# A decoder block's value projection in seven products instead of eight, with weight sums by adding DMAs

## The chip, the cores and the metric

The kernel runs on one core of a Trainium2 chip. The metric is the device time of the program in microseconds. Engines of a core: TensorE (PE, with its weight loads shown as PEld), VectorE (DVE), ScalarE (ACT), GpSimd (POOL) and the queue engine SyncE (SP), which here only issues DMAs.

## The reference

One layer with 512 tokens of width 1024, in float32. A combined input projection `h @ w_in` feeds three groups of heads: A, six heads of dilated attention; B, four heads of gated linear attention in chunks; C, six heads of block-sparse attention.

```
h = RMSNorm(x)
aq, ak, av, bq, bk, bv, br, ba, cq, ck, cv = split(h @ w_in)
y_a = dilated_attention(aq, ak, av)        # 6 heads of 64
y_b = gla(bq, bk, bv, br, ba)              # 4 heads; output gate: norm(o) * silu(br)
y_c = moba_attention(cq, ck, cv)           # 6 heads of 64
x = x + concat(y_a, y_b, y_c) @ w_out
x = x + relu(RMSNorm(x) @ w_ff1)^2 @ w_ff2
out = RMSNorm(x)
```

The part that the change touches is the projection to the values and to the gate, `h @ [av | br half 0]` and `h @ [cv | br half 1]`: 512 tokens by 1024 inputs by two groups of 512 columns (384 of values and 128 of gate each). RMSNorm's row factor (rstd) is applied to the result, and the norm's weights to x.

## The kernel before

Every large product is done in three: both operands are split into a rounded part and a remainder (`xh`, `xl` for x; `wh`, `wl` for a weight piece of 128 rows by 1024 columns), and high times high, low times high and high times low are added in PSUM. ACT makes the rounded part, DVE the remainder (`parts`, line 284; `cut`, line 302, goes through the pieces in the order in which they are fetched). SP fetches them (`fetch`, line 268) and also the bias rows of the softmax (`nb`, `attention`, line 721).

The program is in stages. `first` (line 533) projects group B's q, k, v and low-rank gate. Then `main` (line 1331) runs `v_proj(0)` (values of A and half of the gate), three `qk_proj` pairs, `v_proj(1)` (values of C, the other half), three more pairs, the out-projection, and a feed-forward part in which every unit is done in Strassen's form: seven products of halves instead of eight (the table `PRODUCTS`), with the sums of weights made by DMAs that add to what lies in SBUF (issued by POOL) or by DVE. Beside `main` run `gla` (line 550), `attention` and `values` (line 784), which fill in between.

`v_proj(g)` (line 858) waits for four weight pieces, and for each of four token tiles adds 8 x 3 products of 128x512 into one of the two "mm" banks (`vps`). `v_out` (line 843) reads it twice on ACT: values `v`, and gate `rg`, from which DVE makes `sg` and `rg`; `gate` (line 919) turns them into the swish gate.

In `gla`, `levels` makes for seven block lengths L = 64, 32, ..., 1 an array `kq`; the products of its blocks (`lp`, two levels at a time, in the banks s, s, pt, pt) are copied into `attn` under a mask by DVE (`copy_predicated`). `carry` has two small PE steps, `dps` (read into `dg` by ACT) and `ktp` (the transposed keys, read into `kend`), both in "mm" banks. Then come per chunk the state update `up`, in bank g, and the output `op`, in bank o. `zps` is the gate's low-rank product, from `alT`, the transposed projection.

The order of all instructions is set by `Plan` (line 107): every stream of work is a generator that yields instructions, waits for named events, and takes and gives back resources (PSUM banks by tag, `raw` slots for fetched pieces, `w` for split pairs, `big` for 4 KB buffers). The planner keeps a clock for each engine by rough costs and always issues the instruction that could start first, with a priority for ties. What it decides is a fixed order on each engine; at run time every engine goes through its own in order and waits on semaphores.

In the profile every instruction has the planner's line 129, so groups are told apart by tile names.

Of the kernel before, what the change touches and what calls it, by code (L numbers as in the profile page):

```python
# [9 lines left out]
F32 = mybir.dt.float32  # L10
# [189 lines left out]
def hybrid_block_kernel(ctx: ExitStack, tc: tile.TileContext, xT_d, x_d, w0_d, wv_d, wqk_d, wo_d, w1_d, w2_d,  # L200
# [9 lines left out]
    plan = Plan(nc, dict(BANKS, raw=3, w=WPAIRS, big=BIGS, raw2=3, part=5, lev=4, cnt=1))  # L210
# [28 lines left out]
    nw2 = consts.tile([128, KT], F32)  # L239
    hsel = consts.tile([128, 4], F32)  # L240
# [21 lines left out]
    loaded = {}  # L262
    raws = {}
# [4 lines left out]
    def fetch():  # L268
        for key, src, n in pieces:
            if key[0] == "x":  # L270
                yield SP.dma_start(xT[key[1]], src)
                fire(("x", key[1]))
                continue
            if key[0] == "x3":
                x3[key[1:]] = slot("x3")
                yield SP.dma_start(x3[key[1:]], src)
                continue
# [24 lines left out]
    def cut():  # L302
        for key, src, n in pieces:
            if key[0] in ("x", "x3"):
                continue
            yield ("wait", ("raw", key))
            yield from parts(key, raws.pop(key), n)
            give("raw")
            give("big")

    units = [(i, c) for c in range(NC) for i in (1, 2)]
# [203 lines left out]
    G = []  # L515
# [34 lines left out]
    def gla():  # L550
# [43 lines left out]
        for l0 in range(0, len(LEVELS), 2):  # L594
# [32 lines left out]
        for n in range(NB):  # L627
            vb = vB[n // 2][:, n % 2, :]
            sold = smk
            if n < NB - 1:  # L630
                yield ("take", "g")
                up = bank("g", "up")
# [6 lines left out]
                give("g")  # L639
# [6 lines left out]
            yield ("take", "o")  # L646
            op_ = bank("o", "op")
# [5 lines left out]
            give("o")  # L653
# [189 lines left out]
    def v_out(g, t, acc):  # L843

        v = vS[g, t] = slot("v", shape=(128, 384))
        yield ACT.activation(v, acc[:, :384], AF.Copy, scale=rstd[:, t:t + 1])
# [3 lines left out]
        yield ACT.activation(rg, acc[:, 384:], AF.Copy, scale=nrstd[:, t:t + 1])  # L850
        give("mm")
        yield ("prio", 2)
        yield DVE.tensor_scalar(sg, rg, 80.0, None, op0=OP.min)
        yield DVE.tensor_tensor(rg, rg, gw[:, cs], op=OP.mult)
        if g and t % 2:
            spawn(gate(t // 2), 2)

    def v_proj(g):
        if not gates:
            gates.extend(tuple(slot(x, shape=(128, 2, 256)) for x in ("sg", "rg")) for _ in range(2))  # L860
        hl = []
        for c in range(4):
            yield ("wait", ("w", ("v", g, c)))
            hl.append(loaded.pop(("v", g, c)))
        for t in range(NT):
            yield ("take", "mm")
            acc = bank("mm", "vps")
            ts = slice(t * 128, (t + 1) * 128)
            for k in range(KT):
                wh, wl = hl[k // 2]  # L870
                w_ = slice((k % 2) * 512, (k % 2) * 512 + 512)
                yield [PE.matmul(acc, xx[:, ts], ww[:, w_], start=(k + j == 0), stop=(k == 7 and j == 2))
                       for j, (xx, ww) in enumerate(((xh[k], wh), (xl[k], wh), (xh[k], wl)))]
                if t == NT - 1 and k % 2:
                    give_w()
            if t == 0:
                yield ("wait", "rstd")
                yield ("wait", "consts")
            spawn(v_out(g, t, acc), 0.5)
# [39 lines left out]
    def gate(i):  # L919
# [10 lines left out]
        G.append(rg.rearrange("p t c -> p (t c)"))  # L930
        if i:
            fire("G")

# [413 lines left out]
    for c in range(4):  # L1347
        piece(("v", 0, c), wv_d[0, c])
    for i in range(2):
        piece(("qk", 0, i), wqk_d[i])  # L1350
    for p in (1, 2):
        for i in range(2):
            piece(("qk", p, i), wqk_d[2 * p + i])
    for c in range(4):
        piece(("v", 1, c), wv_d[1, c])
    for p in range(3, 6):
# [8 lines left out]
    def start():  # L1365
# [9 lines left out]
        yield DVE.tensor_scalar(nw2, nw[:, 1], -0.5, None, op0=OP.mult)  # L1375
        yield ("take", "mm")
# [11 lines left out]
    for k in range(KT):  # L1388
        spawn(scaled_x(k), 2)
    spawn(main(), 9)  # L1390
# [82 lines left out]
```

## Time and profile before

| | |
|---|---|
| median of 3 runs | 580.21 us (579.4 to 581.09) |
| the profiled execution | 579.58 us, span of its records 577.8 us |
| granted clock of TensorE | 0.995 |
| PE busy | 566.3 us, 98% |
| DVE busy | 446.6 us, 77% |
| ACT busy | 346.7 us, 60% |
| POOL busy | 53.6 us, 9% |

Stages by the records: the first projection to 29.4 us; `vps` of `v_proj(0)` from 33.5 to 64.7, with the first levels between; `qkps` of three pairs to 115.7; `vps` of `v_proj(1)` to 147.3; three pairs to 198.5; out-projection to about 250; the feed-forward part to the end. The page gives busy shares over the whole span; the answers by window give them for one stage. A matmul's length is its time in the pipeline, 0.39 us for 512 columns, and neighbours overlap, so steps are taken from one start to the next.

### The profile page before, as it was taken

The numbers are of one execution on the slowest core, as the hardware profiler recorded it, in microseconds if no ns is written. First come the engines' busy times: TensorE is split into PE (matmuls) and PEld (weight loads), VectorE is DVE, ScalarE is ACT, GpSimd is POOL, SyncE is SP. The second block draws the span as 40 slices with busy tenths as digits, with TensorE's granted clock in tenths as the row PEclk, the third lists the DMA queues.
The fourth block names the chain that finished last, engine by engine and source line by source line (L and its number), as shares of the span: only waits on it lengthen the run. The fifth ranks groups of instructions, "written<-read, shape, count | busy, mean of one in ns | idle before, by whom it ended". The sixth has DMA issues, their size and how long they took to land.

```text
span 577.8 us, 9359 instructions
## 1 busy us (share of the span) xinstructions
PE 566.3 (98%) x3561; PEld 487.3 (84%) x3561; DVE 446.6 (77%) x795; ACT 346.7 (60%) x601; POOL 53.6 (9%) x73
## 2 busy tenths in 40 slices
PE   9999999999999999999999999999999999999994
PEld 8967888768876778889988799988899888999884
DVE  6799976654796843759799797799975799957993
ACT  6563327646666762558785456865467764579543
POOL 4020000000000010011102002021020120011202
PEclk9999999999999999999999999999999999999998
DMA  8922233040423742378977738978269684395812
GB/s 294 399 76 74 74 111 87 23 146 5 129 87 127 274 110 37 133 220 203 205 222 149 183 111 177 296 121 231 86 150 287 149 166 161 110 218 110 147 38 109
DMA packets 27357, 87.16 MB, mean 151 GB/s; under 512 B 3360, under 2 KB 3402, under 8 KB 27312
## 3 DMA queue, kind: packets, MB, share of 16 engines
q1 hardware_dynamic: 19872, 61.15, 31.0%
q0 software_dynamic: 7152, 25.14, 23.9%
q8 instruction: 28, 0.46, 0.3%
q10 hardware_dynamic: 288, 0.27, 0.1%
q14 instruction: 17, 0.14, 0.1%
HBM read 84.42 MB, written 2.13 MB: 150 GB/s over the span
## 4 chain that ended last, share of the span: by engine, by line
PE 85%; DVE 7%; ACT 3%; DMA 2%; issue 1%; ACTq 0%; DVEq 0%
PE f1X L129 13%; PE f2X L129 12%; PE qkps L129 12%; PE vps L129 8%; PE ops L129 7%; PE f1Z L129 7%; PE f2Z L129 6%; PE f1Y L129 3%; PE f2Y L129 3%; PE sps L129 3%; DMA wraw<-in_w 2%; PE po L129 2%; PE ptp L129 2%; PE av L129 2%; DVE wl L129 2%
## 5 line engine op out<-in xcount | busy, mean ns | idle before, releaser
L129 DVE TENSOR_TENSOR wl<-wraw,wh 128x1024 fp32r<-128x1024 f32 (+1 forms) x148 | 175.1, 1192 | 36.4 <-ACT wh L129 35.9
L129 ACT ACTIVATE wh<-wraw 128x1024 fp32r<-128x1024 f32 (+1 forms) x147 | 149.3, 1032 | 51.9 <-DMA wraw<-in_w 17.4
L129 PE MATMUL f1X<-yp,wh 128*128 128x256 f32 x512 | 92.6, 283 | 0.0
L129 POOL DMA_DIRECT2D wraw<-in_w x46 | 40.5, 977 | 468.2 <-DVE wl L129 229.3
L129 PEld LDWEIGHTS f1X<-yp,wh 128*128 128x128 f32 x512 | 80.1, 192 | 0.3
L129 PE MATMUL f1X<-yp,wl 128*128 128x256 f32 x256 | 72.5, 283 | 0.2 <-DVE wl L129 0.2
L129 PE MATMUL f2X<-wl,Ah 128*128 128x512 f32 (+1 forms) x132 | 50.6, 384 | 0.1
L129 PE MATMUL f2X<-wh,Ah 128*128 128x512 f32 (+1 forms) x132 | 50.6, 383 | 0.0
L129 PE MATMUL f2X<-wh,Al 128*128 128x512 f32 (+1 forms) x132 | 50.6, 383 | 0.0
L129 PEld LDWEIGHTS f1X<-yp,wl 128*128 128x128 f32 x256 | 49.1, 192 | 0.4 <-DVE wl L129 0.4
L129 PE MATMUL f1Z<-yp,wh 128*128 128x256 f32 x256 | 46.6, 284 | 0.3 <-DVE yp L129 0.3
L129 ACT ACTIVATE h<-h 128x512 f32<-128x512 f32 x56 | 34.9, 626 | 11.9 <-DVE h L129 11.1
L129 PE MATMUL qkps<-xh,wh 128*128 128x512 f32 x96 | 40.9, 426 | 0.0
L129 PEld LDWEIGHTS f1Z<-yp,wh 128*128 128x128 f32 x256 | 40.0, 192 | 0.5 <-DVE yp L129 0.5
L129 PE MATMUL qkps<-xh,wl 128*128 128x512 f32 x96 | 37.6, 392 | 0.0
L129 PE MATMUL qkps<-xl,wh 128*128 128x512 f32 x96 | 37.5, 391 | 0.0
L129 ACT ACTIVATE P<-P,mn 128x512 f32<-128x512 f32 (+3 forms) x48 | 26.5, 553 | 17.6 <-DVE mn L129 17.6
L129 ACT ACTIVATE Ah<-h 128x512 fp32r<-128x512 f32 x40 | 24.2, 620 | 20.5 <-DVE h L129 20.5
L129 PE MATMUL f1Z<-yp,wl 128*128 128x256 f32 x128 | 36.2, 283 | 0.0
L129 DVE TENSOR_TENSOR Al<-h,Ah 128x512 fp32r<-128x512 f32 x40 | 26.9, 685 | 4.0 <-ACT Ah L129 4.0
L129 PEld LDWEIGHTS f2X<-wl,Ah 128*128 128x128 f32 x132 | 24.8, 188 | 5.4 <-DVE wl L129 0.5
L129 PEld LDWEIGHTS f2X<-wh,Ah 128*128 128x128 f32 x132 | 24.8, 188 | 4.8
(226 smaller groups left out, 1200.2 us busy)
## 6 DMA issues: line engine op xcount, KB each, us to landing
wraw<-in_w SPq DMA_DIRECT2D x66, 512.0 KB, 4.4
wraw<-in_w POOLq DMA_DIRECT2D x46, 512.0 KB, 6.4
wraw<-in_wqk SPq DMA_DIRECT2D x12, 512.0 KB, 6.6
wraw<-in_wv SPq DMA_DIRECT2D x8, 512.0 KB, 6.7
wraw<-in_wo SPq DMA_DIRECT2D x8, 512.0 KB, 5.8
nb<-tab SPq DMA_DIRECT2D x12, 256.0 KB, 4.0
wraw<-in_w SPq DMA_DIRECT2D x8, 264.0 KB, 6.7
xT<-in_xT SPq DMA_DIRECT2D x8, 256.0 KB, 6.7
```

What stands on the lines that cost most here:

```text
L129: getattr(getattr(self.nc, op.eng), op.method)(*op.args, **op.kw)
```

## The change

The two `v_proj` become one, in Strassen's form with the table that the feed-forward part has: x halved by tokens (256) and by inputs (512), the weights by inputs and by group. Seven products of 2 x 4 x 3 matmuls take the place of eight. Stage order: first, qk pairs 0 and 1, values and gate, qk pairs 2 to 5.

- The sums of x (`x_sums`, new) are made by ACT and DVE in "big" buffers and split into `xsh` and `xsl`.
- The sums of weights are made by POOL's adding DMAs: `fetch_v` loads ten pieces, `v_plus` adds eight times, `cut_v` splits fourteen.
- `v_out` adds products into `v` on DVE, or starts it on ACT, and makes the gate's two arrays from the finished `v`.
- `copy_predicated` is kept for L <= 16; for L = 64 and 32 ACT copies the blocks, one or two instructions for each head.
- `up` and `op` take "pt" banks instead of g and o, since the products hold o and g.

```
@@ gla
-                    yield DVE.copy_predicated(o4, mk, src)
+                    if L >= 32:
+                        for j in range(m):
+                            rows = slice(2 * L * j, 2 * L * j + L)
+                            yield ACT.activation(o4[rows, :, j], src[rows, :, j], AF.Copy)
+                    else:
+                        yield DVE.copy_predicated(o4, mk, src)
...
-                yield ("take", "g")
-                up = bank("g", "up")
+                yield ("take", "pt")
+                up = bank("pt", "up")
...
-            yield ("take", "o")
-            op_ = bank("o", "op")
+            yield ("take", "pt")
+            op_ = bank("pt", "op")
@@ new functions
+    def v_plus(n, ip, t, q):
+        yield POOL.dma_start(t, wv_d[q[1], 2 * q[0] + ip], accum_op=OP.add)
+        VB[n, ip] = t
+        fire(("vB", n, ip))
+
+    def fetch_v():
+        for n, q, more in ((0, (0, 0), None), (1, (1, 0), None), (3, (0, 0), (0, 1)), (5, (1, 1), None), (4, (0, 1), (1, 1))):
+            for ip in range(2):
+                yield ("take", "rawv")
+                yield ("take", "big")
+                VB[n, ip] = t = big("wraw")
+                yield SP.dma_start(t, wv_d[q[1], 2 * q[0] + ip])
+                if more:
+                    spawn(v_plus(n, ip, t, more), 3)
+                else:
+                    fire(("vB", n, ip))
+
+    def cut_v():
+        for n, *_ in PRODUCTS:
+            if n == 2:
+                yield ("prio", 1.5)
+            for ip in range(2):
+                yield ("wait", ("vB", n, ip))
+                t = VB[n, ip]
+                yield from parts(("v", n, ip), t)
+                if n in (3, 2):
+                    spawn(v_plus(*((2, ip, t, (1, 1)) if n == 3 else (6, ip, t, (1, 0)))), 3)
...
+    def x_sums():
...
+        for m in range(4):
+            yield ACT.activation(block(s, m), xT[4 + m][:, 256:], AF.Copy, scale=nnw[:, 4 + m:5 + m])
+        for m in range(4):
+            yield DVE.scalar_tensor_tensor(block(s, m), xT[m][:, 256:], nw[:, 0, m:m + 1], block(s, m), op0=OP.mult, op1=OP.add)
+        yield from parts_of(3, s)
...
@@ v_out
+            yield DVE.scalar_tensor_tensor(v, acc, (nrstd if g else rstd)[:, t:t + 1], v, op0=OP.mult, op1=OP.add)
...
+        yield DVE.tensor_scalar(sg, v[:, 384:], -1.0, 80.0, op0=OP.mult, op1=OP.min)
+        yield DVE.scalar_tensor_tensor(rg, v[:, 384:], -1.0, gw[:, cs], op0=OP.mult, op1=OP.mult)
@@ main
-        yield from v_proj(0)
-        yield from qk_proj(0)
-        yield from qk_proj(1)
-        yield from qk_proj(2)
-        yield from v_proj(1)
-        for p in range(3, 6):
+        for p in range(2):
+            yield from qk_proj(p)
+        yield from v_proj()
+        for p in range(2, 6):
             yield from qk_proj(p)
```

How the instructions stand now, at the places of which the prediction speaks. DVE, where the low-rank gate of group B is made (`la` is the log of the gate, `b` its running sum, from which the levels start); before:

```order
L129 TENSOR_SCALAR Rn_96<-rps 128x512
L129 COPY vals<-vt 12x320
L129 COPY alT<-alps 16x512
L129 COPY vals<-vt 12x320
L129 TENSOR_TENSOR wl<-wraw,wh 128x1024
L129 TENSOR_SCALAR la<-zps,bav 128x512
L129 TENSOR_TENSOR kB<-bk,R 128x512
L129 SCALAR_TENSOR_TENSOR qB<-bq,R 128x512
L129 TENSOR_TENSOR wl<-wraw,wh 128x1024
L129 TENSOR_TENSOR la<-la,ab 128x512
L129 SCALAR_TENSOR_TENSOR b<-smask,la 128x512
```

and after:

```order
L129 COPY alT<-alps 16x512
L129 TENSOR_TENSOR tq<-qkps,Rn_97 128x512
L129 TENSOR_TENSOR wl<-wraw,wh 128x1024
L129 TENSOR_TENSOR q_535<-tq,q_535 128x512
L129 TENSOR_SCALAR la<-zps,bav 128x512
L129 TENSOR_TENSOR kB<-bk,R 128x512
L129 SCALAR_TENSOR_TENSOR qB<-bq,R 128x512
L129 TENSOR_TENSOR la<-la,ab 128x512
L129 TENSOR_TENSOR wl<-wraw,wh 128x1024
L129 TENSOR_TENSOR tk<-qkps,R 128x512
L129 SCALAR_TENSOR_TENSOR b<-smask,la 128x512
```

The reads of the first qk pair (`tq`, `q`, `tk`) now stand between; ahead of this piece stand the sums of x as well.

ACT, between the levels' exponentials `e` and `dg`; before:

```order
L129 ACTIVATE eq<-b 128x512
L129 ACTIVATE e<-e 128x512 x2
L129 ACTIVATE dg<-dps 128x16
L129 ACTIVATE e<-e 128x512
L129 ACTIVATE v<-vps,rstd 128x384
L129 ACTIVATE rg<-vps,nrstd 128x128
L129 ACTIVATE kend<-ktp 128x384
```

and after:

```order
L129 ACTIVATE e<-e 128x512
L129 ACTIVATE attn_596<-lp 64x4x64
L129 ACTIVATE attn_597<-lp 64x4x64
L129 ACTIVATE attn_598<-lp 64x4x64
L129 ACTIVATE attn_599<-lp 64x4x64
L129 ACTIVATE attn_596<-lp 32x4x32 x2
L129 ACTIVATE attn_597<-lp 32x4x32 x2
L129 ACTIVATE attn_598<-lp 32x4x32
L129 ACTIVATE e<-e 128x512
L129 ACTIVATE attn_598<-lp 32x4x32
L129 ACTIVATE attn_599<-lp 32x4x32 x2
L129 ACTIVATE dg<-dps 128x16
```

The twelve copies of the first two levels stand ahead of `dg`.

SP, from the end of the first projection's loads on; before:

```order
L129 DMA wraw<-in_wv 128x1024 x4
L129 DMA wraw<-in_wqk 128x1024 x6
L129 DMA wraw<-in_wv 128x1024
L129 DMA nb<-tab 128x512 x2
L129 DMA wraw<-in_wv 128x1024 x3
```

and after:

```order
L129 DMA wraw<-in_wqk 128x1024 x4
L129 DMA wraw<-in_wv 128x1024 x10
L129 DMA wraw<-in_wqk 128x1024 x3
L129 DMA nb<-tab 128x512 x6
L129 DMA wraw<-in_wqk 128x1024 x5
```

The bias rows `nb` of the first three pairs stand behind all loads for the values and three of the next qk pieces.

More of the change, by code (lines that the diff above doesn't have):

```diff
@@ L262, in hybrid_block_kernel @@
     loaded = {}
+    VB = {}
     raws = {}
@@ L276, in fetch @@
                 yield SP.dma_start(x3[key[1:]], src)
+                continue
+            if key == "v":
+                yield from fetch_v()
                 continue
@@ L305, in cut @@
                 continue
+            if key == "v":
+                yield from cut_v()
+                yield ("prio", 3)
+                continue
             yield ("wait", ("raw", key))
@@ L514, in hybrid_block_kernel @@
     st = {}
-    G = []
+    G = {}
+    gated = [0, 0]
     mh, ml = [None] * 8, [None] * 8
@@ L652, in gla @@
             yield DVE.tensor_tensor(oB[n // 2][:, n % 2, :], op_[:, :256], dv.rearrange("p h v -> p (h v)"), op=OP.add)
-            give("o")
+            give("pt")
         yield ("wait", "G")
@@ L841, in dense, with v_out @@
                    for j, (ww, xx) in enumerate(((wh, ah[k]), (wh, al[k]), (wl, ah[k])))]
-    def v_out(g, t, acc):
-        v = vS[g, t] = slot("v", shape=(128, 384))
-        yield ACT.activation(v, acc[:, :384], AF.Copy, scale=rstd[:, t:t + 1])
+    def v_out(n, q, acc):
+        b_, targets = next((p[1], p[3]) for p in PRODUCTS if p[0] == n)
+        blk, g = targets[0]
+        t = 2 * blk + q
+        if (g, t) not in vS:
+            v = vS[g, t] = slot("v")
+            yield ACT.activation(v, acc, AF.Copy, scale=rstd[:, t:t + 1])
+            done = n == 6
+        else:
+            v = vS[g, t]
+            yield DVE.scalar_tensor_tensor(v, acc, (nrstd if g else rstd)[:, t:t + 1], v, op0=OP.mult, op1=OP.add)
+            done = True
+        if n == 6:
+            give("mm")
+        elif n == 5:
+            give("og"[q])
+        else:
+            fire(("vread", b_, q))
+        if not done:
+            return
         fire(("v", g, t))
@@ L856, in v_out, with v_proj @@
+        gated[t // 2] += 1
+        if gated[t // 2] == 4:
             spawn(gate(t // 2), 2)
[L858 to L879, printed above, removed]
+    def v_proj():
+        gates.extend(tuple(slot(x, shape=(128, 2, 256)) for x in ("sg", "rg")) for _ in range(2))
+        bk = {}
+        yield ("wait", "rstd")
+        yield ("wait", "consts")
+        for n, b_, first_, _ in PRODUCTS:
+            for q in range(2):
+                if n == 0:
+                    yield ("take", "mm")
+                    bk["X", q] = bank("mm", "vps")
+                elif n == 1:
+                    yield ("take", "og"[q])
+                    bk["Y", q] = bk["Z", q] = bank("og"[q], "vps")
+                else:
+                    key = ("vread", "Y" if n == 3 else b_, q)
+                    yield ("wait", key)
+                    plan.done.pop(key)
+                acc = bk[b_, q]
+                ts = slice(q * 128, q * 128 + 128)
+                if n in (2, 3, 4, 5):
+                    yield ("wait", ("xs", n))
+                for ip in range(2):
+                    yield ("wait", ("w", ("v", n, ip)))
+                    wh, wl = loaded["v", n, ip]
+                    for i in range(2):
+                        m = 2 * ip + i
+                        if n in (2, 3, 4, 5):
+                            ah, al = (x[:, m * 256:(m + 1) * 256] for x in XS[n])
+                        else:
+                            k, tok = (m if n == 0 else 4 + m), (256 if n == 6 else 0)
+                            ah, al = (x[k][:, tok:tok + 256] for x in (xh, xl))
+                        ws = slice(i * 512, i * 512 + 512)
+                        yield [PE.matmul(acc, aa[:, ts], ww[:, ws], start=first_ and m + j == 0, stop=(m == 3 and j == 2),
+                                         skip_group_check=True) for j, (aa, ww) in enumerate(((ah, wh), (al, wh), (ah, wl)))]
+                    if q:
+                        give_w()
+                if q and n in (2, 3, 4, 5):
+                    give("xp")
+                    give("big")
+                    give("big")
+                spawn(v_out(n, q, acc), 0.5)
@@ L1346, in hybrid_block_kernel @@
             piece(("x", k + 1), xT_d[k + 1])
[L1347 to L1351, printed above, removed]
+    for p in range(2):
         for i in range(2):
             piece(("qk", p, i), wqk_d[2 * p + i])
-    for c in range(4):
-        piece(("v", 1, c), wv_d[1, c])
-    for p in range(3, 6):
+    piece("v", None)
+    for p in range(2, 6):
         for i in range(2):
@@ L1375, in start @@
         yield DVE.tensor_scalar(nw2, nw[:, 1], -0.5, None, op0=OP.mult)
+        yield DVE.tensor_scalar(nnw, nw[:, 0], -1.0, None, op0=OP.mult)
         yield ("take", "mm")
```

53 lines of the change are left out of this document (44 added, 9 removed).

## The prediction

> **What bounds the kernel now.** The page comes first: how busy each engine is, and the chain that ended last.
>
> ```profile
> PE 566.3 (98%) x3561; PEld 487.3 (84%) x3561; DVE 446.6 (77%) x795; ACT 346.7 (60%) x601; POOL 53.6 (9%) x73
> PE 85%; DVE 7%; ACT 3%; DMA 2%; issue 1%; ACTq 0%; DVEq 0%
> ```
>
> TensorE (PE) is busy 98% and is 85% of the chain. An average says little of one stage, so the stages come next (start:end, length, busy time of PE, PEld, DVE, ACT, POOL, clock, DMA).
>
> ```profile
> 24.70:44.50 19.80, 19.02 (x116) 14.54 (x115) 18.27 (x39) 11.35 (x21) 2.97 (x6) 1.00 0.39 136
> 44.50:74.00 29.50, 28.90 (x306) 23.91 (x303) 27.72 (x67) 11.85 (x20) 0.00 (x0) 1.00 0.22 72
> 74.00:115.00 41.00, 41.00 (x233) 32.68 (x232) 27.29 (x85) 21.99 (x56) 0.00 (x0) 1.00 0.26 78
> 115.00:147.00 32.00, 32.00 (x179) 24.12 (x177) 17.71 (x49) 17.86 (x40) 0.00 (x0) 1.00 0.28 90
> 147.00:200.00 53.00, 53.00 (x299) 39.13 (x297) 41.16 (x107) 35.74 (x78) 0.00 (x0) 1.00 0.45 147
> ```
>
> From 74 to 200 us PE has no idle time. From 24.7 to 74 VectorE (DVE) is nearly as full as PE: 18.27 + 27.72 of 49.3 us. That is where the change puts work on DVE. What PE waited for between 24 and 216 us (in total, times, longest):
>
> ```profile
> PE vps L129 <- ACT rg L129: 0.6, 1, 0.6
> PE alps L129 <- ACT vB L129: 0.5, 1, 0.5
> PE zps L129 <- DVE alT L129: 0.3, 1, 0.3
> ```
>
> So 1.4 us of waits in all. From the long run of out-projection products on (215.9 us) every engine's instructions stand in the same order before and after. A gain or loss made before that point therefore reaches the end unchanged, and the question is only when PE gets there.
>
> **What is removed from PE.** The chain in order of time has a stretch of undisturbed vps products (start, length, what):
>
> ```profile
> 136.41 10.91 PE vps L129 x48
> ```
>
> That is 10.91 / 48 = 0.227 us per product of 512 columns. Before there are 2 x 4 x 8 x 3 = 192 of them; after 7 products x 2 halves x 4 x 3 = 168, of the same shape. 24 x 0.227 = **5.45 us less** on the engine that sets the end. Nothing else on PE changes in number.
>
> **What is added on DVE, and the first wait.** DVE gets 6 more weight remainders (wl, 14 pieces for 8), 16 sums of 256 columns (xs), their remainders (xsl), and 6 more reads of a product; it loses 8 masked copies. By the windows it is idle 41.6 of the 155.5 us from 44.5 to 200, and the additions are some 19 us (priced below: 6 x 1.15 + 16 x 0.36 + 3 x 1.15 + 4 x 0.36 + 6 x 0.66 - 2.7), so they fit on the whole. It needn't fit at each place. The first place is the first product of the gated attention's levels (lp). It needs kq of level 32, and ahead of that row DVE has, from ss on, the following rows of the timeline to price (start, length; the step from one start to the next counts, since neighbours overlap by about 0.08):
>
> ```profile
> 24.70 0.16 DVE L129 TENSOR_SCALAR ss<-rsp 128x4 f32<-128x4 f32 x1 [3.44 <-PE rsp L129]
> 27.60 0.87 DVE L129 TENSOR_SCALAR diag<-cst,rstd 128x128 f32<-128x128 f32 x4
> 28.80 0.66 DVE L129 TENSOR_SCALAR alr<-av,rstd 128x16 f32<-128x16 f32 x4 [0.33 <-PE av L129]
> 31.73 0.47 DVE L129 COPY vals<-vt 12x320 f32<-12x320 f32 x1
> 35.51 0.68 DVE L129 TENSOR_TENSOR kB<-bk,R 128x512 f32<-128x512 f32 x1
> 36.11 0.68 DVE L129 SCALAR_TENSOR_TENSOR qB<-bq,R 128x512 f32<-128x512 f32 x1
> 38.55 1.23 DVE L129 TENSOR_TENSOR_SCAN b<-smask,la 128x512 f32<-128x512 f32 x1
> 39.81 0.76 DVE L129 TENSOR_TENSOR e<-b 128x256 f32<-128x256 f32 x2
> 44.16 0.42 DVE L129 TENSOR_TENSOR kq<-qB,e 128x256 f32<-128x256 f32 x1
> 59.28 2.35 DVE L129 TENSOR_TENSOR wl<-wraw,wh 128x1024 fp32r<-128x1024 f32 x2
> ```
>
> ss runs at 24.70 as before, since it waits for PE. Then: 9 remainders of 1024 columns at 1.15 (10.4), 14 rows of 512 at 0.61 (8.5), 8 of 256 at 0.34 (2.7), 11 xs, the scan (1.3), and diag, alr, vals and single columns (2.7). An xs row of 256 columns in three operands isn't in the trace: it lies between 0.34 (two operands, 256) and 0.60 (512); I take 0.36, next to the row of its own length, so 4.0. The sum is 29.6 us: lp can start at 24.7 + 29.6 = **54.3** (before it ended this row at 44.5).
>
> PE reaches that lp so (start, length):
>
> ```profile
> 29.44 1.02 PE L129 MATMUL rps<-diag,ones 128*128 128x512 f32 x2
> 33.52 0.79 PE L129 MATMUL vps<-wh,xh 128*128 128x512 f32 x1
> 43.57 2.18 PE L129 MATMUL lp<-kq 32*128 32x64 f32 x64
> 46.49 0.95 PE L129 MATMUL dps<-hsel,qk 128*128 128x4 f32 x8
> 48.07 0.49 PE L129 MATMUL ktp<-cst,ek 128*128 128x128 f32 x3
> ```
>
> It is free at 29.44, has the small products that took from there to the first vps (4.1 us, less the 0.8 of waits at alps and zps: 3.3), and 87 qkps products at 0.227 (19.8): 52.5. The waits of alps and zps stay about as they were, since alT now stands 7 us later but behind 30 qkps products: 0.9 for 0.8 us. So PE is there at 53.4 and **waits 0.9 us**. Bounds: none, if an xs costs 0.34 and the DVE rows leave no gap; 3 us, if DVE waits in the longer stretch as it did in the shorter (19.80 - 18.27 = 1.5 us before, half as long again now, on top of 0.9).
>
> **The two copied levels.** 8 masked copies leave DVE and 12 copies arrive on ScalarE (ACT). Rows: the masked copies as a group, three of the removed ones, and on ACT a copy of 256 columns from PSUM with the row behind it, two copies of 512, and dg.
>
> ```profile
> L129 DVE COPY_PREDICATED attn<-lmask,lp 128x256 f32<-128x256 int32 x28 | 12.2, 531 | 1.6 <-PE lp L129 1.6
> 49.91 1.10 DVE L129 COPY_PREDICATED attn<-lmask,lp 128x256 f32<-128x256 int32 x3
> 93.23 0.37 ACT L129 ACTIVATE th<-ptp 128x256 f32<-128x256 f32 x1
> 93.50 1.05 ACT L129 ACTIVATE wh<-wraw 128x1024 fp32r<-128x1024 f32 x1
> 94.44 1.08 ACT L129 ACTIVATE th<-ptp 128x512 f32<-128x512 f32 x2
> 47.47 0.18 ACT L129 ACTIVATE dg<-dps 128x16 f32<-128x16 f32 x1 [1.56 <-PE dps L129]
> ```
>
> DVE loses 8 x 0.34 = 2.7 us. Copies on part of the partitions aren't in the trace. A copy of 256 columns is 0.37 long but the next row starts 0.27 behind it, so I take 0.28; two of 512 take 1.08, 0.5 a step, so 256 columns fewer save about 0.22 and 128 columns take about 0.17. 4 x 0.28 + 8 x 0.17 = 2.5 us; the upper end is 12 x 0.37 = 4.4. These copies are not free: behind them on ACT stand an e (0.52) and dg (0.18), and dg empties the PSUM bank that ktp is written to. From the end of lp PE has 9 qkps (2.0) and dps (0.8) to do, 2.8 us; ACT needs 2.5 + 0.5 + 0.2 = 3.2 and a hand-over of 0.1. **ktp waits 0.5 us** (0 to 2.4). Before, dg came right behind dps.
>
> **Two more hand-overs.** The next three lp each use the four banks of the one before. DVE clears them of levels 4 and 2 with 8 masked copies and one product read in between: 8 x 0.47 + 0.66 = 4.4 us (0.47 is between the 0.34 of early rows and the 0.531 mean), against 18 vps products, 4.1 us: 0.4 us (0 to 1). Then "up" takes a pt bank, where before it had g: it waits for three masked copies of level 1 (1.7 us), which stand behind 2 pairs of gate rows (0.8) and a wl (1.15), against 9 vps products and lp (3.0): 0.6 us (0 to 1.5). The first vps no longer waits for rg (0.6 us gone).
>
> **The weight sums.** 8 adding DMAs go on POOL's queue, 10 loads instead of 8 on SP's.
>
> ```profile
> wraw<-in_w POOLq DMA_DIRECT2D x46, 512.0 KB, 6.4
> nb<-tab SPq DMA_DIRECT2D x12, 256.0 KB, 4.0
> L129 POOL DMA_DIRECT2D wraw<-in_w x46 | 40.5, 977 | 468.2 <-DVE wl L129 229.3
> ```
>
> A sum of this kind lands 6.4 us after its issue, and POOL spends 0.98 us on each. The sum for product 2 starts when DVE has cut piece (3, 1), near 72 us, lands near 80, and PE wants it near 90: hidden with 8 to 10 us to spare, behind vps products. On SP the first nb rows now stand behind all ten wv and three wqk loads. The last of these gets its buffer when PE has done 66 vps products, near 82 us; nb lands near 87 and the softmax wants it near 91. Nothing, with 4 us to spare.
>
> **Sum.** The profiled execution took 579.58 us (span 577.8). -5.45 + 0.9 + 0.5 + 0.4 + 0.6 - 0.6 + 0.1 = -3.55: 576.0 us. The median shown is 580.21, 0.63 above this execution, so I predict 576.7. With every wait gone, the 1.4 us of before too, it is 580.21 - 5.45 - 1.4 = 573.4; with every one at its upper end (3 + 2.4 + 1 + 1.5 - 0.6 + 0.1 = 7.4) 582.2.
>
> **Rivals.**
> 1. DVE keeps up and nothing new waits: 580.21 - 5.45 = 574.8. For it: DVE has 42 us idle from 34 to 200. Against it: from 24.7 to 74 DVE is already 93% busy. 15%.
> 2. The waits take the place of the products: with the first lp at 2.5 us and ktp at 1.5 the sum is -5.45 + 2.5 + 1.5 + 0.4 + 0.6 - 0.5 = -0.95, 579.3. For it: DVE rows are priced without gaps. 25%.
> 3. Slower: DVE becomes the bound of the vps stretch itself. Rows for it: DVE and PE on the softmax tiles P of all six pairs (as a window), and PE pieces of the chain.
>
> ```profile
> 80.00:216.00 136.00, 16.76 (x120) 14.31 (x120) 35.26 (x86) 33.39 (x106) 1.00 0.36 115
> 126.02 1.00 PE sps L129 x12
> 133.96 0.87 PE ptp L129 x8
> 80.47 1.32 PE op L129 x10
> ```
>
> A pair's softmax is (35.26 - 86 x 0.08) / 6 = 4.7 us on DVE, 6 with its reciprocals. From "up" to the last wl of the values the order has two of them (12), six wl (6.9), five xsl and four xs rows (3.9), three reads of products (2.0) and a dozen gated rows of 256 columns (4.1): 29 to 30 us. Until PE needs that wl it has 84 vps (19.1), 48 sps (5.6), 36 ptp (3.9), 20 op and two up (5.7): 34.3 us. Cover: 4.4 us. From 74 to 115 us before, DVE was idle 13.7 of 41 us, mostly waiting for products just made. If it waits so again (a third of 34.3, 11.5 us), PE loses 7 us: 576.7 + 7 = 583.7. It decides from 9.7 us of DVE waits on (4.4 + 3.55 + 1.74). Against it: DVE waits when it is ahead, and here it is behind. 12%.
> 4. A weight sum lands late. The last pieces' sums, 6a, 4b and 6b, follow each other on POOL; 4b lands near 93 and ACT reaches its cut near 98. If each of the first two waits out a pair of wl rows (2.35 us), and 4b's load comes as late again, it lands near 100, and the exponentials queued behind the cut on ACT come 2.4 us late: 579.1. 3%, since POOL issued the 46 sums of the feed-forward part in 0.98 us each beside a busy DVE. [...]
>
> **How the numbers follow.** My forecast has 45%, the rivals 15, 25, 12 and 3%. No change that a measurement of this kernel can tell is about 0.3%, 1.74 us: below 578.47 is faster, above 581.95 slower. Forecast and rival 1 are faster (60%); rivals 2 and 4 are in the middle (28, of which I give 2 to slower, for all waits at their upper ends); rival 3 is slower: 60, 26, 14. The range leaves out about the lowest and the highest tenth: 574.0 to 581.5.
>
> **What would show it.** vps 168 times at 0.227; PE at the long run of ops near 212.4 instead of 215.9. Waits of PE: lp on DVE kq 0.9, ktp on ACT dg 0.5, up or lp on DVE attn 1.0, none over 1 us between 85 and 215. wl of the last value piece done some 4 us ahead of its product. The prediction is wrong if PE waits more than 3 us in all for DVE kq, or if the stretch from 85 to 125 us has PE waits for DVE wl, xsl or P.

## The result

The changed kernel took 577.01 us (median of 8 executions, 575.93 to 578.25), the kernel before 579.94 (8, 579.2 to 581.09): a ratio of 0.995, interval 0.9936 to 0.9964. The forecast was 576.7 in a range of 574.0 to 581.5. The profiled execution took 577.07 us, 2.51 less than that of before.

The page of the changed kernel, engines and chain:

```profile
PE 562.2 (98%) x3537; PEld 483.2 (84%) x3537; DVE 462.8 (80%) x824; ACT 359.5 (62%) x621; POOL 60.5 (11%) x81
PE 87%; DVE 8%; ACT 2%; issue 1%; DMA 1%; SPq 0%; DVEq 0%; ACTq 0%
```

24 matmuls fewer (3537 for 3561), 16 us more on DVE, 13 more on ACT. PE is as full as before. The same five stretches as before (start:end, length, busy time of PE, PEld, DVE, ACT, POOL, clock, DMA):

```profile
24.70:44.50 19.80, 18.42 (x90) 14.05 (x89) 18.40 (x39) 11.54 (x18) 4.73 (x8) 1.00 0.57 167
44.50:74.00 29.50, 28.53 (x261) 23.33 (x259) 27.00 (x56) 17.15 (x35) 1.77 (x2) 1.00 0.42 91
74.00:115.00 41.00, 40.97 (x298) 32.73 (x291) 38.48 (x109) 25.60 (x58) 3.52 (x4) 1.00 0.61 157
115.00:147.00 32.00, 32.00 (x175) 24.13 (x175) 28.58 (x62) 21.88 (x40) 0.00 (x0) 1.00 0.40 145
147.00:200.00 53.00, 52.34 (x304) 38.12 (x302) 37.30 (x113) 35.93 (x85) 0.00 (x0) 1.00 0.42 140
```

The DVE column is the one to read: 38.48 of 41 us from 74 to 115, where it had 27.29. And yet PE stands still only 0.03 us there; all its waits lie elsewhere:

```profile
PE qkps L129 <- DVE Rn L129: 1.0, 1, 1.0
PE ktp L129 <- ACT dg L129: 1.0, 1, 1.0
PE ptp L129 <- DVE P L129: 0.7, 1, 0.7
PE rps L129 <- DVE vals L129: 0.2, 1, 0.2
```

That is 2.9 us between 24 and 216, where there were 1.4. The long run of out-projection products, the place from which on nothing differs (chain of waits: before, then after):

```profile
215.91 15.88 PE ops L129 x69
```

```profile
213.66 15.91 PE ops L129 x69
```

2.25 us earlier. But in this execution the first projection also ended later, its last bk product starting at 30.16 us in place of 29.20. One difference stands in ACT's rows: the second piece of x arrived at 7.27 us, where ACT was at it at 5.23 before.

```profile
7.27 0.72 ACT L129 ACTIVATE xh<-xT,nw 128x512 fp32r<-128x512 f32 x1 [2.38 <-DMA xT<-in_xT]
```

Up to there the engines and queues stand in the same order as before, but for one small row more on DVE (nnw). Whether that piece is the whole reason is not shown: in the kernel "xsl later" below, ACT was at it at 5.05 us, and the last bk product still came at 29.94. From the end of the first projection to the long run it is 186.71 us before and 183.50 after: **3.21 us** less, and that is what the change did in these two executions. It adds up so: -5.45 for the products, +1.5 for the waits (2.9 less 1.4), and +0.8 for changes of kind. The last is seen wherever vps products follow something else:

```profile
116.30 0.47 PE L129 MATMUL vps<-wh,xh 128*128 128x512 f32 x1
116.61 0.39 PE L129 MATMUL vps<-wh,xl 128*128 128x512 f32 x1
116.84 0.39 PE L129 MATMUL vps<-wl,xh 128*128 128x512 f32 x1
117.07 0.38 PE L129 MATMUL ptp<-cst,P 128*128 128x128 f32 x2
```

The first product behind a ptp takes 0.31 us to the next start, the others 0.23. Work of other streams (lp, up, op, sps, ptp) now cuts the vps products into 18 runs, before into 13, and both ends of a run are slow: its first product takes some 0.12 us more than 0.227, its last some 0.05. The steps of all vps come to 46.0 us before and 41.4 after, 4.6 less and not 5.45.

### The profile page after: what moved, and what is told of

Read it like the earlier page. It is cut to its first block, busy times and chain, and to the rows that moved or that the text cites. A ratio compares the mean times of both kernels' runs of the same rounds, so it can differ in the third digit from the quotient of the medians.

```text
span 575.3 us, 9397 instructions
## 1 busy us (share of the span) xinstructions
PE 562.2 (98%) x3537; PEld 483.2 (84%) x3537; DVE 462.8 (80%) x824; ACT 359.5 (62%) x621; POOL 60.5 (11%) x81
## 4 chain that ended last, share of the span: by engine, by line
PE 87%; DVE 8%; ACT 2%; issue 1%; DMA 1%; SPq 0%; DVEq 0%; ACTq 0%
PE f2X L129 15%; PE f1X L129 15%; PE qkps L129 8%; PE f2Z L129 8%; PE ops L129 7%; PE f1Z L129 7%; PE vps L129 7%; PE f2Y L129 4%; PE f1Y L129 3%; PE sps L129 3%; PE ptp L129 2%; PE po L129 2%; DVE wl L129 2%; PE av L129 1%; DMA xT<-in_xT 1%
## 5 line engine op out<-in xcount | busy, mean ns | idle before, releaser
L129 DVE TENSOR_TENSOR wl<-wraw,wh 128x1024 fp32r<-128x1024 f32 (+1 forms) x154 | 182.3, 1192 | 36.0 <-ACT wh L129 35.7
L129 ACT ACTIVATE wh<-wraw 128x1024 fp32r<-128x1024 f32 (+1 forms) x153 | 156.1, 1032 | 55.5 <-DMA wraw<-in_w 17.6
L129 ACT ACTIVATE h<-h 128x512 f32<-128x512 f32 x56 | 34.9, 626 | 11.7 <-DVE h L129 10.9
L129 ACT ACTIVATE junk<-x 128x512 f32<-128x512 f32 (+1 forms) x17 | 10.3, 605 | 29.7 <-DVE x L129 29.7
```

The costliest lines, as they stand in the source:

```text
L129: getattr(getattr(self.nc, op.eng), op.method)(*op.args, **op.kw)
```

## Experiments

Twelve kernels, in three groups; the kernel before ran beside each group (579.85, 580.10 and 579.81 us). The first is the changed kernel unaltered. Nine keep its planner's order, with an instruction held back, exchanged, made twice or left out at the moment at which it is written out. The last two are the kernel before with one part of the change, planned anew. The table has the medians and, from each profile, the distance from the last bk product of the first projection to the long run of ops, which leaves out the start; then the waits of PE that differ from the changed kernel, and how long the clock was at 0.50 between the start and the long run (worked out from the windows of granted clock: the time missing from 1.00, doubled).

| kernel | median, us | distance, us | waits of PE, us | clock low, us |
|---|---|---|---|---|
| before | 579.94 | 186.71 | rg 0.6, alps 0.5, zps 0.3 | none |
| the change | 577.01 | 183.50 | Rn 1.0, dg 1.0, P 0.7, vals 0.2 | none |
| the change once more | 576.24 | 183.50 | the same | none |
| dg first | 575.88 | 182.98 | dg 0, tk 0.5 | none |
| dg first, tk first | 575.99 | 183.02 | dg 0, tk 0.5 | none |
| xsl later | 577.72 | 185.20 | Rn 0.7, dg 1.5 | 3.4 |
| both moves | 575.91 | 183.11 | Rn 0.7, dg 0.2, tk 0.5 | none |
| copies on DVE | 581.01 | 189.76 | dg 0.8, tk 1.4 | 10.2 |
| no sums | 576.37 | 183.52 | the same | none |
| copies twice | 577.92 | 189.18 | tk 0.8, dg 0.8 | 10.2 |
| three remainders more | 579.28 | 185.86 | scores 1.9 more | none |
| eight remainders more | 586.06 | 192.20 | scores 4.1, up 1.3, lp 0.2 more | 3.4 |
| order alone (on before) | 592.29 | 198.19 | lp 3.2, P 0.7, ml 0.4, Rn 0.3 | 17.1 |
| ACT copies alone (on before) | 580.56 | 187.35 | rg 0.9, alps 0.5, zps 0.3 | none |

### The changed kernel once more

> The changed kernel once more, unaltered. In the first profile of it TensorE was done with the first projection 0.96 us later than in the kernel before (first vt at 30.40 us against rps at 29.44), because the second xT piece arrived at 7.2 us in place of 5.2. Theory A (the start varies from one execution to the next and has nothing to do with the change): another profile ends the first projection anywhere between 29.4 and 30.5, and the wait for Rn (1.0) and for dg (1.0) are there again at the same size; time 576.4 to 577.6. Rival B (the change makes the start late): again near 30.4.

576.24 us (5 executions, 575.59 to 577.35; ratio to before 0.9941, 0.9929 to 0.9953). The waits are the same four to 0.01 us. The first projection ended at 29.65 us; in the profiles of all 14 kernels of this study it lay between 28.80 and 30.16, with the three of the old kernel and its variants at 29.20, 29.45 and 29.88. So theory A holds: the start varies by over 1 us, and the first profile's late start wasn't the change's. The distance is again 183.50 us.

### dg ahead of the copies of L = 32

```
-  ACT: attn(64) x4, attn(32) x5, e, attn(32) x3, dg, wh
+  ACT: attn(64) x4, e, dg, attn(32) x8, wh
```

> Only ScalarE's order is altered: dg (and one e) stand ahead of the eight copies of L = 32 instead of behind them. Theory A (the wait of ktp, 0.97 us, is dg standing behind the copies, and nothing else is short there): the wait for dg falls under 0.2, the following lp comes some 0.8 earlier, and the time is 0.7 to 1.0 us less than that of the changed kernel (576.0 to 576.3 on its 577.0). Rival B (VectorE or the copies bind the next lp anyway): lp waits in place of ktp, for attn copies or kq, and the time is within 0.3 of the changed kernel.

575.88 us (575.56 to 576.28; ratio 0.9934, 0.9922 to 0.9945): 0.36 less than the kernel of the same comparison. The waits:

```profile
PE qkps L138 <- DVE Rn L138: 1.0, 1, 1.0
PE ptp L138 <- DVE P L138: 0.7, 1, 0.7
PE vps L138 <- DVE tk L138: 0.5, 1, 0.5
PE rps L138 <- DVE vals L138: 0.2, 1, 0.2
```

The wait for dg is gone, so its cause was the queue on ACT, as both theories had it; but half of it came back one product later, as a wait for tk. The distance is 0.52 us shorter, not 0.97. Neither expectation had this: not lp waits, but vps.

### tk ahead of a wl, on top of it

```
-  DVE: e x2, wl (1,1), tk, kq
+  DVE: e x2, tk, wl (1,1), kq
```

> As the kernel with dg ahead of the copies of L = 32, and on VectorE the wl of piece (1, 1) behind tk of pair 1 instead of ahead of it. With dg first, vps waited 0.46 us for tk, which stood behind that wl (1.2 us). Theory A (the gain of dg was half eaten by this one neighbour): no wait at ktp nor at that vps, 0.9 to 1.0 us less on TensorE up to the first up than in the changed kernel, 575.2 to 575.6. Rival B (another wait takes its place at lp or later): as with dg alone, 575.9, with a wait at lp for attn or kq.

575.99 us (575.60 to 576.25; ratio 0.9928, 0.9916 to 0.9940): the same as with dg alone, and the wait for tk is still there. PE, and the row of DVE:

```profile
60.26 0.49 PE L138 MATMUL ktp<-cst,ek 128*128 128x128 f32 x3
61.21 0.50 PE L138 MATMUL vps<-wh,xh 128*128 128x512 f32 x1 [0.46 <-DVE tk L138]
```

```profile
60.46 0.69 DVE L138 TENSOR_TENSOR tk<-qkps,R 128x512 f32<-128x512 f32 x1 [1.73 <-PE qkps L138]
```

tk now starts as soon as the last qkps product is through, with DVE idle 1.73 us ahead of it. It empties the bank that vps wants: with two mm banks, one holding dps and the other the keys' product, ktp and vps need both within 0.3 us. So the wait is one reading of a bank, 0.69 us, less the 0.3 of ktp, and no order on DVE removes it. My reading of the run before, that the wl was at fault, was wrong.

### The second xsl behind the first levels

```
-  DVE: wl, xsl, Rn, alT, ... kq (32), e
+  DVE: wl, Rn, alT, ... kq (32), xsl, e
```

> Only VectorE's order is altered: the second xsl (1.21 us, the remainder of the sums for product 5) stands behind the kq of level 32 instead of ahead of Rn. Theory A (the wait for Rn, 1.02 us, is that one instruction, and what comes later on VectorE has room): the wait for Rn falls to 0.2 or less, no lp waits, and the time is 0.8 to 1.1 us less than that of the changed kernel. Rival B (VectorE is full from 25 to 74 us, so each us moved behind the first lp comes up as a wait at a later lp, up or vps): a wait of 0.5 us or more stands at lp or at vps between 57 and 90 us, and the time is at most 0.5 less.

577.72 us (8 executions, 576.05 to 579.49; ratio 0.9964, 0.9950 to 0.9979): slower than the changed kernel by about 1.5. But the eight fall in two halves: four with a mean clock of 0.997 or 0.998 took 576.05 to 577.28 us, as the changed kernel did (575.59 to 577.35 when it was run once more), and four with 0.994 or 0.995 took 578.16 to 579.49, the profiled one among them. The wait for Rn fell only to 0.7, since Rn now finds rps not yet read, and DVE is idle 0.71 us ahead of it. And xsl, now behind kq, delays the e after it by 0.8 us against the end of the first projection; ACT does that level's e ahead of the copies, and starts them and dg 0.2 later, while PE comes 0.3 sooner. So the gap at ktp grows by half a us. What then happens on PE:

```profile
61.81 0.86 PE L138 MATMUL ktp<-cst,ek 128*128 128x128 f32 x3 [1.49 <-ACT dg L138]
62.32 0.77 PE L138 MATMUL vps<-wh,xh 128*128 128x512 f32 x1
62.89 0.63 PE L138 MATMUL vps<-wh,xl 128*128 128x512 f32 x1
63.32 0.63 PE L138 MATMUL vps<-wl,xh 128*128 128x512 f32 x1
```

The products behind the gap take 0.43 us a step, nearly twice their 0.227. The windows (the third number from the end is the granted clock):

```profile
60.00:62.00 2.00, 0.51 (x3) 0.20 (x2) 2.00 (x4) 1.93 (x7) 0.00 (x0) 0.97 0.00 0
62.00:65.00 3.00, 3.00 (x9) 2.11 (x8) 2.56 (x6) 2.11 (x4) 0.00 (x0) 0.50 0.00 0
```

After a gap of 1.49 us the clock was 0.50 for 3.4 us, which costs half of that, 1.7, and the distance grew by 1.7; the waits themselves came to only 0.2 us more (0.5 at ktp, less 0.3 at Rn). So what makes this kernel slower is the clock, in the executions where it falls. Rival B's word, that moved work comes up as a wait elsewhere, is right, though by way of ACT.

### Both moves

> Both moves in one kernel: dg ahead of the copies of L = 32 on ScalarE and the second xsl behind the kq of level 32 on VectorE. Theory A (two separate waits): the gains add, 1.6 to 2.0 us less than the changed kernel, 575.0 to 575.4. Rival B (VectorE is the bound up to the fourth lp): the two together give no more than one alone, 576.0 or more, with a new wait at the second or third lp.

575.91 us (6 executions, 575.22 to 577.78; ratio 0.9939, 0.9925 to 0.9953): what dg brings alone. Waits: Rn 0.7, tk 0.5, dg 0.2 and the rest as they were. The clock stays at 1.00. The gains don't add.

### The two levels back on DVE

```
-  ACT.activation(o4[rows, :, j], src[rows, :, j], AF.Copy)      # 12
+  DVE.copy_predicated(o4, mk, src)                              # 8, at the place of the first copy of each
```

> The changed kernel with the two levels L = 64 and 32 copied under the mask by VectorE, as before: eight masked copies where the twelve copies of ScalarE began, all else in the same order. Theory A (ScalarE's copies were worth their wait: VectorE has only 0.6 us free between the first and the second lp, so 8 x 0.34 = 2.7 us come up as about 2.1 us of wait for tk and kq): ktp no longer waits for dg (0.97 less), vps or lp wait 1.5 to 2.3 for VectorE, 0.5 to 1.3 us slower than the changed kernel (about 577.5), and up to 1.6 more where the clock drops. Rival B (VectorE had room, and the copies on ScalarE only brought the wait for dg): 0.5 to 1.0 us faster than the changed kernel, 575.5 to 576.

581.01 us (12 executions, 577.70 to 582.86; ratio 1.0005, 0.9985 to 1.0025): the gain of the whole change is gone. PE waits, and the clock behind them:

```profile
PE vps L136 <- DVE tk L136: 1.4, 1, 1.4
PE ktp L136 <- ACT dg L136: 0.8, 1, 0.8
```

```profile
62.00:64.00 2.00, 1.56 (x5) 1.33 (x6) 2.00 (x6) 1.26 (x3) 0.00 (x0) 0.80 0.00 0
64.00:70.00 6.00, 6.00 (x70) 4.95 (x69) 3.91 (x9) 0.38 (x1) 1.77 (x2) 0.50 0.43 66
```

The two waits come to 2.2 us where there was 0.97, 1.2 more, and the clock is low from 63.2 to 73.5, which costs 5.1 us: together 6.3, the growth of the distance. Theory A had the wait for tk (1.4, forecast 1.5 to 2.3), but not that dg is still awaited: the e ahead of it on ACT now comes at 59.69 us, after 3.6 us of waiting for DVE. It also took the clock to cost 1.6 at most. Of the twelve, four had a mean clock of 0.997 or 0.998 and took 577.7 to 578.1 us: 1.5 to 1.9 slower than the changed kernel, about the price of the waits alone. Of the seven at 580.6 and above, five had 0.987, one 0.991 and one 0.994. So the ACT copies are needed: with these copies on DVE, tk comes too late where PE needs two banks. In the median, though, most of the loss is the clock's.

### No weight sums

> The changed kernel without the eight adding DMAs: the weight sums are left out, and the products of 3, 4, 2 and 6 use single pieces; order and all other work are the same. Theory A (the sums are hidden: a piece's wl was done 3.8 us or more ahead of its first product): within 0.4 us of the changed kernel. Rival B (the adding DMAs and POOL's issues take time from VectorE or from the loads): 1 us or more faster.

576.37 us (4 executions, 575.62 to 578.10; ratio 0.9942, 0.9924 to 0.9959), the changed kernel's 576.24. Waits and distance are the same to 0.02 us. No cost of the eight adding DMAs shows.

### Four copies of L = 32 made twice

> The changed kernel with four of the copies of L = 32 issued twice on ScalarE (same data, 4 x 0.27 = 1.1 us more ahead of dg), all else the same. Theory A (a wait of TensorE costs its own length): the wait at ktp grows from 0.97 to 2.05, and the time by 1.0 to 1.1, 577.3 on the 576.2 of the same comparison. Rival B (a gap of TensorE of about 1.5 us or more brings the granted clock to 0.50 for some 3 us, as in the kernel with xsl behind kq): the first vps behind ktp take 0.43 us each in place of 0.23, and the time grows by 2.4 to 3, about 578.6 to 579.2, in most executions.

577.92 us (12 executions, 576.58 to 583.05; ratio 0.9971, 0.9952 to 0.9991). In the profile ktp waits 0.79 us for tk and the vps behind it 0.83 for dg, 1.62 in all where it was 0.97. Then:

```profile
60.00:62.00 2.00, 0.89 (x5) 0.61 (x6) 1.64 (x5) 1.93 (x7) 0.00 (x0) 1.00 0.00 0
62.40:72.64 10.24, 10.24 (x80) 8.23 (x80) 5.17 (x12) 2.78 (x7) 1.77 (x2) 0.50 0.58 101
```

Half speed from 62.4 to 72.6 us. Six executions had a mean clock of 0.997 or 0.998 and took 576.6 to 578.2 us (theory A); two had 0.987 and took 581.2 and 583.1, the profiled one among them; the four between had 0.995, 577.6 to 579.0. So the same kernel has a low mean clock in some executions and not in others, and rival B's "in most" was wrong.

### Three, then eight remainders made twice

```
+  DVE: wl (5,1) x2, wl (2,0) x2, wl (2,1) x2                                        # load3
+  DVE: wl x2 for (3,1), (5,0), (5,1), (2,0), (2,1), (4,0), (4,1), (6,0)             # load8
```

> The changed kernel with the remainders wl of pieces (5, 1), (2, 0) and (2, 1) made twice on VectorE (same data, 3 x 1.15 = 3.45 us more between 83 and 95 us), all orders else the same. In the changed kernel the smallest lead of a wl over its first product behind that place is 3.8 us, at (4, 1), and 3.9 at (6, 1). Theory A (the lead is what covers it): no more than 0.5 us slower than the changed kernel, 576.2 to 576.8, with the lead of (4, 1) at about 0.4. Rival B (VectorE sets the pace there already through the softmax): TensorE waits for P or sps, 2 us or more slower. Rival C (VectorE's idle time takes it all): the lead stays at 3 us or more.

> The same with eight remainders made twice, (3, 1) to (6, 0): 7 x 1.15 = 8.05 us more on VectorE ahead of the wl of (4, 1) or with it. Theory A (a lead of 3.8 us, then each us counts, less what idle time of VectorE takes up: it was idle 3.2 us from 85 to 125): TensorE waits 1 to 4.5 us for wl, P or softmax tiles between 85 and 125, 577.5 to 581, more if a single wait is long enough to bring the clock down. Rival B (VectorE was the bound already): 8 us or more slower. Rival C (not on the path at all): the same as the changed kernel.

579.28 us with three (10 executions, 578.0 to 580.33; ratio 0.9989, 0.9979 to 0.9998), 586.06 with eight (4, 584.66 to 587.67; ratio 1.0108, 1.0086 to 1.0130): some 3 and 10 us slower than the changed kernel. With three, PE waits 1.9 us more for the scores, in two waits, and the longer is:

```profile
97.00 0.44 PE L135 MATMUL sps<-k,q 64*128 64x384 f32 x1 [1.68 <-DVE mn L135]
```

sps, the softmax scores, want the banks s back, which DVE frees when it has read the scores before (mn is what that reading leaves). DVE's rows show that a doubled wl takes 2.48 us, and one alone 1.22, so 3.8 us were added, not 3.45. 1.9 came up as waits, and the distance grew by 2.4 (0.5 of it is not placed): the room is **2 us at the most**, 1.4 by the distance, and it is at the scores, not at the weights. The wl of (4, 1) still led by 3.79 us and that of (6, 1) by 3.86, because DVE's row there stands behind scores that PE itself makes: PE and DVE are late together. With eight:

```profile
83.95 0.70 PE L135 MATMUL up<-vB,kend 128*128 128x256 f32 x2 [1.26 <-DVE attn L135]
99.62 0.44 PE L135 MATMUL sps<-k,q 64*128 64x384 f32 x1 [2.93 <-DVE mn L135]
118.53 0.83 PE L135 MATMUL sps<-k,q 64*128 64x256 f32 x6 [0.84 <-DVE mn L135]
```

```profile
101.32:104.73 3.41, 3.41 (x8) 2.71 (x9) 2.00 (x9) 3.32 (x10) 0.00 (x0) 0.50 0.57 112
```

The clock fell behind the 2.93 us here; behind the 1.68 of the run with three it stayed at 1.00. Rival B was nearest to both. For the 10.1 us added (eight times 1.26) there are 5.6 us of waits and 1.7 for the clock (half of 3.4); the distance grew by 8.7, so 1.4 us are not placed.

### The order of stages alone

```
@@ the kernel before
-  v_proj(0), qk 0, 1, 2, v_proj(1), qk 3, 4, 5
+  qk 0, 1, v_proj(0), v_proj(1), qk 2, 3, 4, 5
```

> The kernel before with the new order of stages alone: first, pairs 0 and 1, values of A, values of C (eight products, no sums), pairs 2 to 5; copies and banks as before. Theory A (the gain is the 24 products; the order alone gives nothing): not faster than the kernel before. In the order that the planner makes, the second lp, dps, ktp and the third lp follow each other on TensorE without products between, so TensorE waits there some 2 to 4 us for dg and for the eight masked copies, and the clock may drop behind: 580.5 to 586. Rival B (the order of stages is the gain, the products are eaten by waits): 578 or less.

592.29 us (4 executions, 591.62 to 594.07; ratio 1.0219, 1.0200 to 1.0239): 12 us slower than before. The products of the levels now follow each other:

```profile
59.79 2.65 PE L129 MATMUL lp<-kq 32*128 32x64 f32 x58 [1.32 <-DVE attn L129]
62.37 1.87 PE L129 MATMUL dps<-hsel,qk 128*128 128x4 f32 x8
64.10 0.88 PE L129 MATMUL ktp<-cst,ek 128*128 128x128 f32 x3
64.91 4.41 PE L129 MATMUL lp<-kq 32*128 32x64 f32 x64
71.16 3.63 PE L129 MATMUL lp<-kq 32*128 32x64 f32 x32 [1.83 <-DVE attn L129]
```

```profile
62.00:76.00 14.00, 12.17 (x116) 11.03 (x113) 10.90 (x23) 2.72 (x5) 0.00 (x0) 0.50 0.13 39
```

3.2 us more of waits in all, and half speed from 60.9 to 78 us, which costs 8.5: 11.7 of the 11.5 us by which the distance grew. The second is much the larger. So the new order is no gain by itself; in the changed kernel qkps and vps products stand between the levels' products. (This isn't the changed kernel less the seven products: the planner orders it anew. That the gain is the 24 products rests on the sum of steps and waits in the records above, not on a run that changes them alone.)

### The ACT copies alone

```
@@ the kernel before
-  yield DVE.copy_predicated(o4, mk, src)                        # L = 64, 32
+  yield ACT.activation(o4[rows, :, j], src[rows, :, j], AF.Copy)
```

> The kernel before with the copies of L = 64 and 32 on ScalarE and nothing else (the planner then also puts ktp behind the second lp). Theory A (VectorE isn't awaited there in the kernel before, so 2.7 us off it bring nothing): within 1 us of the kernel before, 579.2 to 581. Rival B (the copies are a gain by themselves): 578.5 or less. Rival C (dg behind the copies costs as in the changed kernel): 581 or more.

580.56 us (10 executions, 579.79 to 585.11; ratio 1.0031, 1.0008 to 1.0053). No gain, as theory A said: in the kernel before PE hardly waited for DVE there. The distance is 0.6 us longer. One wait is longer, 0.93 us in place of 0.60:

```profile
49.84 0.50 PE L129 MATMUL vps<-wh,xh 128*128 128x512 f32 x1 [0.93 <-ACT rg L129]
```

and two of the ten took 584.7 and 585.1 us at a mean clock of 0.988.

## Why the prediction was right, step by step

**The time.** 576.7 forecast, 577.01 and 576.24 measured, -3.55 us forecast and -3.21 measured from the end of the first projection. That it came so near is in part luck, because several terms erred and nearly cancelled. Against the forecast, the products brought 0.8 us less, the first wait cost 0.4 more and ktp 0.5 more, and 0.7 at ptp was not foreseen: 2.4 to the bad. The waits at alps and zps, which I had kept at 0.9, were gone (alT was done at 40.8 us, and zps came at 41.8), and the fourth lp and up cost nothing in place of 1.0: 1.9 to the good. Neither sign of being wrong came: PE never waited for kq, and between 85 and 125 us it waited for no wl, xsl or P.

**The products.** 168 in number, 0.227 us undisturbed, but -4.6 in place of -5.45: the step "24 x 0.227, nothing else on PE changes" left out that the vps products are cut into more runs, 18 for 13, at some 0.17 us each.

**The first wait.** Forecast 0.9 us at the first lp, for kq; it came as 1.02 + 0.24 at Rn and rps, 15 us earlier. The sum of DVE rows was good: 29.6 us from ss to the second level, 30.3 measured (25.66 to 55.94; an xs took 0.40 a step, not 0.36). What failed is the place: I looked only for the end of the row, and PE meets this queue at the first product that needs anything from it. Having waited for Rn, PE reached lp 0.3 us ahead of the last kq, which the lp of the level before it covers.

**ktp.** Forecast 0.5, measured 0.97. The copies:

```profile
L129 ACT ACTIVATE attn<-lp x12: 262/268/378, 57.7 to 61.3; 32x128 f32<-32x128 f32 x8, 64x256 f32<-64x256 f32 x4
57.75 2.45 ACT L129 ACTIVATE attn<-lp 64x256 f32<-64x256 f32 x9 [0.47 <-PE lp L129]
...
60.74 0.82 ACT L129 ACTIVATE attn<-lp 32x128 f32<-32x128 f32 x3
61.59 0.18 ACT L129 ACTIVATE dg<-dps 128x16 f32<-128x16 f32 x1
```

A copy of 128 columns on 32 partitions takes 0.27 us, not 0.17: the twelve took 3.2 us (57.75 to 61.59 less the e between them), not 2.5. The mechanism was right, and the run with dg first shows it; its gain is only half, since with two mm banks the reading by tk is due at the same place.

**The fourth lp and up.** Forecast 0.4 and 0.6; neither waited. DVE's side was priced well:

```profile
75.38 3.21 DVE L129 COPY_PREDICATED attn<-lmask,lp 128x256 f32<-128x256 int32 x7 [0.80 <-PE lp L129]
79.59 1.37 PE L129 MATMUL lp<-kq 32*128 32x64 f32 x32
83.27 0.70 PE L129 MATMUL up<-vB,kend 128*128 128x256 f32 x2
```

The eight masked copies and the read took 4.4 us (75.38 to 79.75), as forecast, at 0.33 us a copy in the first five and up to 0.6 in the rest; the gate rows, the wl and the next three copies took 3.7 (79.56 to 83.22), also as forecast. The step that failed is PE's time: the 18 vps took 4.3 us (75.29 to 79.59), not 4.1, and the nine vps with lp 3.7 (79.59 to 83.27), not 3.0, so the banks were free when PE came.

**What wasn't forecast.** ptp waits 0.66 us at 192.9, in pair 5, far behind the change:

```profile
191.63 0.69 DVE L129 TENSOR_TENSOR tk<-qkps,R 128x512 f32<-128x512 f32 x1 [0.27 <-PE qkps L129]
192.24 0.21 DVE L129 RECIPROCAL rz<-z 128x1 f32<-128x1 f32 x2
192.43 0.62 DVE L129 TENSOR_SCALAR P<-P,rz 128x256 f32<-128x256 f32 x2
```

The softmax's last two rows stand behind tk, which waits for the product that PE has only just finished. The order is the planner's; it was not run another way, so what another order would bring is not shown.

**The weight sums.** As forecast: the wl of the last value piece was done at 115.45 us and its first product came at 119.32, 3.9 us later; POOL issued its eight in 0.86 to 1.24 us each, and without them the time is the same (576.37 and 576.24 us). Rival 4 did not come: from 85 to 125 us PE was busy 40.00 of 40 us, and the issues of the last three sums took 1.77 us for two and 0.87 for the third, with DVE busy 36.77 of those 40.

**The rivals.** Rival 1 fell: there were new waits. Rival 2's waits came to a third of its price. Rival 3, DVE as the bound of the vps stretch, did not happen, but I gave it a cover of 4.4 us, worked out at the last wl, and the run with three remainders doubled shows 2 at the most: the scores' banks are tighter than the weights. With that it decides from 2 + 3.2 + 1.74 = 6.9 us on, not from 9.7. The 12% rested on too wide a margin.

## What to carry to other kernels

Where an engine is in order and nearly full, ask not only when its row of work ends but which product of PE meets that row first, and count banks there: two readings that free two banks are one wait (with dg first, the 0.97 us at ktp went, and 0.46 came at the vps behind it). Before calling a cover so and so long, look for the tightest link of all that the loaded engine serves; here the scores had 2 us at the most where the weights had 3.8. And a wait of PE can have a second price beside its length, the clock behind it: in "xsl later" 0.2 us more of waits came with 3.4 us at a clock of 0.50, which cost 1.7.

## What the runs showed of the hardware

A short gap of PE can cost several times its length: in "order alone" a gap of 1.32 us stands ahead of a stretch at half speed that cost 8.5. Behind gaps of 1.49 us, of 2.93, of 0.79 + 0.83 and 0.76 + 1.45 (ktp between) and of 1.32 us the granted clock was 0.50, for 3.4, 3.4, 10.2, 10.2 and 17.1 us: one, one, three, three and five times 3.4. Behind the gap of 0.97 it stayed at 1.00 in all five profiles that have it, and behind the one of 1.68 us as well. The kernel with the copies doubled took 576.6 us in one execution, at a mean clock of 0.997, and 583.1 in another, at 0.987.

The length of the gap alone does not decide (the clock fell behind 1.32 us and stayed behind 1.68); the traces point to where it falls. In the traces the clock changes on a grid of 3.41 us: from the first record of the full clock to the drop there are 54.61, 58.03, 58.03, 95.57 and 54.61 us (xsl later, copies on DVE, copies twice, eight remainders, order alone), which is 16, 17, 17, 28 and 16 times 3.41; to the drop at the very end there are 566.61 us before and 563.20 after the change, 166 and 165 times 3.413. So PE's work is counted here in the step of this grid ahead of each drop, and in those where a long gap had no such effect:

| kernel | step of the grid, us | PE busy, us of 3.41 | clock behind it |
|---|---|---|---|
| copies on DVE | 59.81 to 63.22 | 1.33 | 0.50 |
| eight remainders more | 97.91 to 101.32 | 1.53 | 0.50 |
| copies twice | 58.99 to 62.40 | 1.79 | 0.50 |
| xsl later | 58.48 to 61.89 | 1.92 | 0.50 |
| order alone (lp for the most part) | 57.47 to 60.88 | 2.09 | 0.50 |
| dg first, tk first | 36.64 to 40.05 | 2.03 | 1.00 |
| three remainders more | 92.92 to 96.34 | 2.39 | 1.00 |
| three remainders more | 96.34 to 99.75 | 2.58 | 1.00 |
| the change | 58.26 to 61.67 | 2.60 | 1.00 |

The gap of 1.68 us lies across two steps, and neither is left as empty as those ahead of a drop. In the steps of the table without lp, the clock fell behind 1.33 to 1.92 us of work and stayed behind 2.03 to 2.60. The low clock lasted more than one step only where products of levels followed (lp, 64 columns on 32 rows): every low step that was followed by another had lp in it, and the last of each low stretch at most 0.3 us of it. None of the five steps ahead of a drop was without work: PE was busy for 1.33 to 2.09 us of each, and the longest gap was 2.93 us.

Why the clock stayed low for three and five steps where lp followed, and fell behind the 2.09 us of "order alone", is not shown: lp was not tried apart. Three of the 17 executions of the changed kernel, the repeated one and the one without sums took 578.1 to 578.3 us, the other 14 575.6 to 577.4. Whether the clock fell in those is not known, since none of the three was profiled. Their mean clock, 0.995, does not tell: in every profile the clock is 0.50 at the very end as well, for 2.6 us (three remainders more, mean 0.998) to 5.5 us (before, mean 0.995), while a drop of 3.4 us takes 0.003 off the mean; an execution of the changed kernel at 575.93 us had 0.995 too. With dg first, which leaves no gap above 1.02 us, the ten executions of those two kernels lay between 575.56 and 576.28; with both moves, which leave no gap above 0.7, five of six lay between 575.22 and 576.34, and one took 577.78.

The three kernels with dg first are the fastest that were run, 575.88, 575.91 (both moves) and 575.99 us against 576.24 in the first comparison; the intervals of their ratios overlap that of the changed kernel, so the difference of the medians is not shown. The spread is narrower in two of the three.
